# Reordering the gate entry, moving weight sums from GpSimd to VectorE, and another order for the output rows in a Winograd-multiplied transformer block

## The chip, the core and the metric

The kernel runs on one core of one Trainium2 chip. The core has five instruction streams that the profile names PE (TensorE, matrix products), DVE (VectorE, elementwise work), ACT (ScalarE, elementwise functions and casts), POOL (GpSimd, elementwise work) and SP (SyncE, which here issues the DMAs). Each works through its own list in order; they wait for each other through semaphores. The metric is the device time of one execution in microseconds (us), the median of several. The time before is 942.32 us (three runs, 941.96 to 943.43).

## The reference

One layer of a diffusion backbone over 1024 tokens with 1024 channels (cut):

```python
h = rms_norm(x, g_pre) * (1 + scale) + shift
q, k, v, g_a, u_f, g_f, c_a, c_b, g_c, s_a, s_f, s_c = split_in(h @ w_in)
attn = neighbourhood_attention(q, k, v, kc, vc, rpb)
y_a = (attn * silu(g_a)) @ p_attn
y_f = ((fourier_mix(u_f) @ w_four) * silu(g_f)) @ p_four
y_c = (conv_module(c_a, c_b, ...) * silu(g_c)) @ p_conv
merged = sigmoid(s_a) * y_a + sigmoid(s_f) * y_f + sigmoid(s_c) * y_c
x = x + gate * rms_norm(merged @ w_out, g_post)
```

All of it is float32. The change touches the last three stages: the gate products (`h @ w_in` for g_a, g_f, g_c and most of s_a, s_f, s_c), the projections by p_attn, p_four and p_conv with the merge, and the output product by w_out with its normalised rows.

## The kernel before, in words

A float32 product is made of three: each operand is split into a high and a low part in the type fp32r (`split`, L92: ACT casts the high part, DVE or POOL subtracts for the low one), and high x high, high x low and low x high are added up in PSUM (`mm3`). The channels lie on the 128 partitions in 8 tiles, the tokens in two halves of 512 columns.

**Gate stage** (from about 513 us). The weight columns of w_in come in pairs of 2 x 128 columns, `NP` = 12 pairs numbered 0 to 11. Of each pair the weights are a 2 x 2 block matrix a11, a12, a21, a22, and the activations are a 2 x 2 block matrix too, so that Winograd's form of Strassen's method makes the four output blocks from seven products, not eight. A product is 4 k-tiles x 3 = 12 matmuls of 128x512. It takes sums of weight blocks (`wsum`, L1260, tiles named w: w0 = a21+a22, w1 = w0-a11, w2 = a11-a21, w3 = a12-w1) and sums of activations (tiles t, made and split once by `h_sums`, `h_last` and `h_split`). `prep_a` to `prep_d` split a11 and a12, w0 and w1, w2 and w3, and a22, into tiles named c. `step` (L1335) holds the products p1 to p7 and the merges g2, g3, g4, g7:

- p1 fills the PSUM bank x; ACT copies it (s1). p2 fills y; g2 adds s1 and y on DVE.
- p6 adds into x; DVE copies it (u2, L1303). p7 adds into x again, so p7 cannot start before that copy, nor p6 before s1.
- p5 fills z; ACT copies it (s5). p3 adds into z, p4 fills a bank of its own. g7, g3 and g4 add copies and banks on DVE (L1329).

A merged gate goes through a tanh on ACT. The kind of a pair says what follows: for the first five pairs (kind "s") the tanh is stored to memory (`thd`, L1309); for pairs 5 to 7 (kind "g") DVE and POOL (L1325) multiply it into the branch results `mg`; for the last four (kind "a") it is kept in `mg`.

All five engines' orders are written by hand in this part: the order of the calls is the order on each engine. A call such as go(1, "p3", "g3") puts matmuls on PE, a copy on ACT and an addition on DVE at that place of each list. Pairs 0 to 2 are interleaved, as the activation sums become ready; pairs 3 to 11 go through a loop (L1482 and on). The raw weight tiles come through two buffers ("raw"), one for each half of a pair; `raws` issues the loads of the next pair as soon as the buffers' readers are placed. Up to pair 2 `wsum` runs on DVE, from pair 3 to 11 on POOL, after that on DVE.

**Projection** (from about 753 us). For each of 8 output tiles d and both halves h, three products are made; DVE multiplies each by its gate (L1633) and POOL adds the second and third into `mg[d]` (L1636), but for d = 7, h = 1, where DVE adds. Beside it `side` loads, combines and splits the weights w_out (tiles wo) for the last stage and loads the rows of the output gate.

**Output** (from about 843 us). The same seven-product form, with roles swapped: `mg` gives the blocks that are split into c tiles, w_out the sums. Four quarters n = NP to NP+3 of 2 x 128 tokens each. Here the merges are put on a list (`pend`) and `flush` hands them to `emit_out`: ACT squares and sums a row's half, POOL multiplies it by the output gate (L1724) and takes the power -0.5 (L1731), and DVE adds the scaled result to the rows of x (L1738), which SP stores. `x_load` loads those rows.

The end of the projection is written so that a11 of the first quarter is split in the projection's last step and a12 after it, in two pieces, since it needs the last tile of `mg`:

```python
a12 = mgt[1][:, :, 0:P]
dst = [v[:, 4:8] for v in ops["c0"]]
for ks in (slice(0, 3), slice(3, 4)):
    split(a12[:, ks], *(v[:, ks] for v in dst), dve)
```

Of the kernel before, what the change touches and what calls it, by code (L numbers as in the profile page):

```python
# [19 lines left out]
P = 128  # L20
# [32 lines left out]
def block_kernel(ctx: ExitStack, tc: tile.TileContext, x, ctxt, wmodp, wgate,  # L53
# [1206 lines left out]
    def wsum(n, i):  # L1260
        a11, a12, a21, a22 = blocks(n)
        i0, i1, op = ((a21, a22, ALU.add), (ops.get((n, 0)), a11, ALU.subtract), (a11, a21, ALU.subtract),
                      (a12, ops.get((n, 1)), ALU.subtract))[i]
        t = swp.tile([P, 512], F32, tag="sw", name=f"w{i}")
        t = t.rearrange("p (k c) -> p k c", k=4)
        (pool if 2 < n < NP else dve).tensor_tensor(out=t, in0=i0, in1=i1, op=op)  # L1266
        ops[n, i] = t

    def prep_b(n, which=(0, 1)):
# [188 lines left out]
    go(0, "g3")  # L1458
    go(1, "p7")
    prep_b(2, (1, 0))  # L1460
    h_split(4, 0, 1)
    go(0, "g7")
    go(1, "p3", "g3")
    h_last(2)
    h_last(3)
    go(2, "p1", "p2")
    h_split(4, 2, 3)
    go(1, "g7")
    for r in (6, 7, 4, 5, 0, 1):
        sp.dma_start(mg[r], fcd[r])  # L1470
    go(2, "p6", "g2")
# [151 lines left out]
    def project(d):  # L1623
        wh, wl = wget(i_p[d])
        for h in range(2):
            s = H[h]
            thq[d, 0, h] = mg[d][:, s]
            for b, (k0, k1) in enumerate(((0, 4), (4, 6), (6, 8))):
                ps = bank("ps")
                for k in range(k0, k1):  # L1630
                    mm3(ps, wh[:, k], wl[:, k], gh[k][:, s], gl[k][:, s], k == k0, k == k1 - 1)
                t = thq[d, b, h]
                dve.scalar_tensor_tensor(out=t, in0=t, scalar=1.0, in1=ps, op0=ALU.add, op1=ALU.mult)  # L1633
                if b > 0:
                    eng = dve if d == 7 and h == 1 else pool
                    eng.tensor_tensor(out=mg[d][:, s], in0=mg[d][:, s], in1=t, op=ALU.add)  # L1636
            side(d, h)

    def side(d, h):
# [29 lines left out]
        if (d, h) == (7, 0):  # L1669
            wload(7)  # L1670
            c0 = wtile("c0o")
            put(NP, "a11", mgt[0][:, :, 0:P], c0, 0)
            ops["c0"] = c0
            wsum(NP, 2)
        for i in WS.get((d, h), ()):
            wsplit(i)
# [26 lines left out]
    def emit_out(n, i, h, src):  # L1703
# [27 lines left out]
        pool.tensor_tensor(out=rs, in0=v, in1=mhalf, op=ALU.pow)  # L1731
        xt = xts[n, i]

        def end(h, eng=dve):
            s = H[h]
            y = yrow[t, h]
            if eng is dve:
                dve.scalar_tensor_tensor(out=xt[:, s], in0=y, scalar=rs, in1=xt[:, s], op0=ALU.mult, op1=ALU.add)  # L1738
            else:
                act.activation(y, y, AF.Identity, scale=rs)  # L1740
                pool.tensor_tensor(out=xt[:, s], in0=xt[:, s], in1=y, op=ALU.add)
            sp.dma_start(out[t * P:(t + 1) * P, s], xt[:, s])

        end(1 - h)
        if (n, i) == (NP + 3, 0):
            ends.append(lambda: end(h, pool))
            return
        while ends:
            ends.pop()()
        end(h)  # L1750

    ends = []
    n = NP
    a12 = mgt[1][:, :, 0:P]
    dst = [v[:, 4:8] for v in ops["c0"]]
    for ks in (slice(0, 3), slice(3, 4)):
        split(a12[:, ks], *(v[:, ks] for v in dst), dve)
    ops[n, "a12"] = dst
    wsum(n, 0)
    go(n, "p1")  # L1760
    prep_b(n, (0,))
# [27 lines left out]
    go(n, "p4")  # L1789
    prep_c(n + 1)  # L1790
    go(n + 1, "p1")
    flush()
    prep_d(n + 1)
    for n in range(NP + 1, NP + 4):
        more = n + 1 < NP + 4
        x_load(n)
        go(n, "p2", "g2")
        go(n, "p6")
        if more:
            prep_a(n + 1)  # L1800
            wsum(n + 1, 0)
            wsum(n + 1, 1)
        flush()
        go(n, "p5")
        go(n, "p7")
        if more:
            prep_b(n + 1)
            wsum(n + 1, 2)
# [10 lines left out]
        if more:  # L1819
            prep_d(n + 1)  # L1820
            go(n + 1, "p1")
        flush()
    allman.close()
    ds.close()
    ms_.close()
# [65 lines left out]
```

## Time and profile before

| what | value |
|---|---|
| median of 3 runs | 942.32 us |
| profiled execution, its own time | 943.67 us |
| its span, first to last instruction | 941.9 us |
| PE busy | 890.4 us, 95% |
| weight loads (PEld) busy | 746.4 us, 79% |
| DVE busy | 725.9 us, 77% |
| ACT busy | 413.8 us, 44% |
| POOL busy | 341.9 us, 36% |
| mean granted TensorE clock | 0.985 |

A row of the timeline gives the start, the duration, the engine, the source line, the operation and the tiles (written <- read), and in brackets how long the engine was idle before it and what ended that. Two operations of one kind that follow each other are merged (x2). A row of a table of stretches gives the stretch, its length, the busy time of the engines asked for with their counts, the granted clock of TensorE, the share of the DMA engines that were busy and GB/s. PE's busy time is modelled: matmuls follow each other closer than their durations say.

### The profile page before, as it was taken

What the parts mean: (1) busy time and instruction counts of PE and PEld (TensorE: products, weight loads), DVE (VectorE), ACT (ScalarE), POOL (GpSimd) and SP (SyncE); (2) the same over time, 40 slices, a digit from 0 to 9 for tenths busy, and PEclk for the clock granted to TensorE, in tenths of its full rate; (3) what the DMA queues carried; (4) which work ended last, traced back from release to release, by engine and by line L of the source; (5) the groups of instructions that cost most, each with busy time, mean ns of one, the idle gap of its engine ahead of it and who ended that gap; (6) DMA issues with size and microseconds to landing.
All of it is one profiled execution on the core that took longest, in us unless ns stands there. A gap on an engine that the chain in (4) does not pass through costs nothing. (4 is left out here: it accounts for less than half of the span.)

```text
span 941.9 us, 13235 instructions
## 1 busy us (share of the span) xinstructions
PE 890.4 (95%) x4652; PEld 746.4 (79%) x4652; DVE 725.9 (77%) x1183; ACT 413.8 (44%) x830; POOL 341.9 (36%) x310
## 2 busy tenths in 40 slices
PE   4899989999899999999999989999999999998896
PEld 2578889988678888888888877788878888775685
DVE  4656897596768999999959786557864679997985
ACT  4344523233456766776643444333343521225441
POOL 2123822164234434444420003335652048570232
PEclk9999989999999999999999999999999999999999
DMA  9703024345434444544323236423313799851323
GB/s 366 277 13 122 23 78 147 112 140 181 119 104 146 135 145 128 162 128 134 124 79 114 72 130 230 126 80 109 112 58 88 245 349 328 288 204 40 109 90 134
DMA packets 114162, 135.85 MB, mean 144 GB/s; under 512 B 5680, under 2 KB 83760, under 8 KB 114096
## 3 DMA queue, kind: packets, MB, share of 16 engines
q1 hardware_dynamic: 113952, 134.43, 43.5%
q0 software_dynamic: 144, 0.59, 0.3%
q8 instruction: 36, 0.59, 0.3%
q14 instruction: 30, 0.25, 0.1%
HBM read 102.03 MB, written 29.36 MB: 139 GB/s over the span
## 5 line engine op out<-in xcount | busy, mean ns | idle before, releaser
L141 PE MATMUL ps<-hh,whi 128*128 128x512 f32 x304 | 126.7, 417 | 0.9 <-DVE qd L851 0.9
L93 POOL TENSOR_TENSOR wlo<-raw,whi 128x512 fp32r<-128x512 f32 (+2 forms) x52 | 79.1, 1539 | 119.5 <-ACT whi L93 107.3
L143 PE MATMUL ps<-hh,wlo 128*128 128x512 f32 x304 | 119.6, 394 | 0.0
L142 PE MATMUL ps<-hl,whi 128*128 128x512 f32 x304 | 119.6, 393 | 0.0
L93 DVE TENSOR_TENSOR c<-w,c 128x512 fp32r<-128x512 f32 x64 | 53.0, 865 | 30.0 <-ACT c L93 29.9
L93 ACT CAST whi<-raw 128x512 fp32r<-128x512 f32 (+2 forms) x65 | 43.8, 705 | 69.7 <-PE ps L142 27.9
L1636 POOL TENSOR_TENSOR mg<-mg,th 128x512 f32<-128x512 f32 x30 | 50.6, 1687 | 62.3 <-DVE th L1633 60.7
L1013 POOL TENSOR_TENSOR bias<-mk,braw 128x288 f32<-128x288 bf16 (+1 forms) x64 | 54.2, 848 | 38.8 <-DVE mn L1045 37.6
L143 PEld LDWEIGHTS ps<-hh,wlo 128*128 128x128 f32 x304 | 57.5, 189 | 12.7
L141 PEld LDWEIGHTS ps<-hh,whi 128*128 128x128 f32 x304 | 57.7, 190 | 11.1 <-PE ps L143 1.3
L142 PEld LDWEIGHTS ps<-hl,whi 128*128 128x128 f32 x304 | 57.8, 190 | 9.7 <-issue 0.5
L1078 ACT CAST pt<-tp 96x384 fp32r<-96x384 f32 (+1 forms) x96 | 46.1, 514 | 43.0 <-PE tp L1071 42.3
L1084 DVE TENSOR_TENSOR pt<-tp,pt 96x384 fp32r<-96x384 f32 (+1 forms) x96 | 54.4, 593 | 2.9 <-ACT pt L1078 1.4
L1045 DVE CUSTOM_DVE_ANT_0 pr<-scb,bias 128x544 f32<-128x544 f32 (+1 forms) x64 | 49.4, 772 | 8.5 <-PE scb L1038 7.7
L1266 POOL TENSOR_TENSOR w<-raw 128x512 f32<-128x512 f32 x9 | 13.8, 1538 | 109.6 <-DMA raw<-in_w_in_dram 99.6
L1052 ACT ACTIVATE pr<-pr,mn 128x544 f32<-128x544 f32 (+1 forms) x64 | 50.8, 794 | 3.7 <-DVE mn L1045 3.6
L143 PE MATMUL ps<-gh,wlo 128*128 128x512 f32 x128 | 50.0, 390 | 0.7 <-DVE wlo L93 0.7
L141 PE MATMUL ps<-gh,whi 128*128 128x512 f32 x128 | 50.3, 393 | 0.0
L142 PE MATMUL ps<-gl,whi 128*128 128x512 f32 x128 | 50.0, 390 | 0.2 <-DVE gl L93 0.2
L1071 PE MATMUL tp<-ident,pr 128*128 128x128 f32 (+1 forms) x320 | 45.8, 274 | 1.4 <-DVE rc L1058 1.0
L93 ACT CAST c<-w 128x512 fp32r<-128x512 f32 x64 | 37.1, 617 | 22.7 <-DVE w L1266 19.5
L141 PE MATMUL x<-t,c 128*128 128x512 f32 x96 | 39.1, 407 | 6.5 <-ACT s L1301 3.3
(498 smaller groups left out, 2639.3 us busy)
## 6 DMA issues: line engine op xcount, KB each, us to landing
raw<-in_w_in_dram SPq DMA_DIRECT2D x51, 512.0 KB
wt<-in_wmodp_dram SPq DMA_DIRECT2D x16, 512.0 KB
thd<-th SPq DMA_DIRECT2D x32, 256.0 KB
th<-thd SPq DMA_DIRECT2D x32, 256.0 KB
braw<-in_rpbp_dram SPq DMA_DIRECT2D x32, 192.0 KB
vt<-vd SPq DMA_DIRECT2D x48, 128.0 KB
vd<-vs SPq DMA_DIRECT2D x20, 256.0 KB
vt<-vd SPq DMA_DIRECT2D x48, 96.0 KB
```

Source lines behind the costliest of these rows:

```text
L93: return act.copy(hi, src), (lo_eng or pool).tensor_tensor(out=lo, in0=src, in1=f32(hi), op=ALU.subtract)
L141: pe.matmul(ps, wh, mh, start=start, stop=False, **kw)
L142: pe.matmul(ps, wh, ml, start=False, stop=False, **kw)
L143: pe.matmul(ps, wl, mh, start=False, stop=stop, **kw)
L1013: pool.tensor_tensor(out=dst, in0=mk[:, a * 3 + MJ[j], 0:n].rearrange("p (r w) -> p r w", w=W), in1=raws[h_, min(j, 1)][:, :, 0:W], op=ALU ...
L1045: dve.tensor_tensor_reduce(out=pr, in0=sc, in1=biases[h_][:, FULL[h_](n)], scale=1.0, scalar=BIG, op0=ALU.add, op1=ALU.min, accum_out=mn)
L1052: act.activation(pr, pr, AF.Exp, scale=-1.0, bias=mn, accum_out=sums)
L1071: pe.transpose(tp[0:(kw if b < 3 else P), b], src, ident)
L1078: act.copy(pt[0:q, b0:b1, 0], tp[0:q, b0:b1])
L1084: dve.tensor_tensor(out=pt[0:q, b0:b1, 1], in0=tp[0:q, b0:b1], in1=f32(pt[0:q, b0:b1, 0]), op=ALU.subtract)
L1266: (pool if 2 < n < NP else dve).tensor_tensor(out=t, in0=i0, in1=i1, op=op)
L1636: eng.tensor_tensor(out=mg[d][:, s], in0=mg[d][:, s], in1=t, op=ALU.add)
```

## The change

Five edits:

1. Gate entry: the call for g7 of pair 0 and p3 of pair 1 goes ahead of the first half of the last activation split; p1 and p2 of pair 2 go ahead of g3 and g7 of pair 1; the second half of that split goes behind g7 of pair 1.
2. `wsum` runs on DVE for every pair.
3. In the projection DVE adds the parts for both halves of d = 7.
4. a12 of the first output quarter is split whole, inside the projection's last step.
5. Output rows: both halves of a row are finished by DVE one after the other; the special path through ACT and POOL for one row of the last quarter is gone; p6 with its copy is called ahead of the merge g2, and `flush` is called behind p6 and p7 and no more behind the next quarter's p1.

```diff
-        (pool if 2 < n < NP else dve).tensor_tensor(out=t, in0=i0, in1=i1, op=op)
+        dve.tensor_tensor(out=t, in0=i0, in1=i1, op=op)
...
     prep_b(2, (1, 0))
+    go(0, "g7")
+    go(1, "p3")
     h_split(4, 0, 1)
-    go(0, "g7")
-    go(1, "p3", "g3")
+    go(2, "p1", "p2")
+    go(1, "g3")
     h_last(2)
     h_last(3)
-    go(2, "p1", "p2")
+    go(1, "g7")
     h_split(4, 2, 3)
-    go(1, "g7")
...
-                    eng = dve if d == 7 and h == 1 else pool
+                    eng = dve if d == 7 else pool
...
             put(NP, "a11", mgt[0][:, :, 0:P], c0, 0)
-            ops["c0"] = c0
+            put(NP, "a12", mgt[1][:, :, 0:P], c0, 1)
             wsum(NP, 2)
...
-        end(1 - h)
-        if (n, i) == (NP + 3, 0):
-            ends.append(lambda: end(h, pool))
-            return
-        while ends:
-            ends.pop()()
-        end(h)
+        for s, y in ((H[v], yrow[t, v]) for v in (1 - h, h)):
+            dve.scalar_tensor_tensor(out=xt[:, s], in0=y, scalar=rs, in1=xt[:, s], op0=ALU.mult, op1=ALU.add)
             sp.dma_start(out[t * P:(t + 1) * P, s], xt[:, s])
...
     go(n + 1, "p1")
-    flush()
     prep_d(n + 1)
     for n in range(NP + 1, NP + 4):
         more = n + 1 < NP + 4
+        go(n, "p2", "p6", "g2")
+        flush()
         x_load(n)
-        go(n, "p2", "g2")
-        go(n, "p6")
         if more:
             prep_a(n + 1)
             wsum(n + 1, 0)
             wsum(n + 1, 1)
-        flush()
         go(n, "p5")
         go(n, "p7")
+        flush()
...
             go(n + 1, "p1")
-        flush()
+        else:
+            flush()
```

The lists of PE and SP keep their order. Three places of the others follow, each a piece of the difference between the two lists (a plus marks a row of the changed kernel, a minus one of the kernel before).

ACT at the gate entry: c are pair 2's weight splits, t the activation split, s the copies of PSUM banks (from x the copy s1 of pair 2, from z the copy s5 of pair 0), th the tanh of a merged gate (of s for g7 of pair 0, of u for g3 of pair 1):

```order
 L93 CAST c_6095<-w_6070 128x512
+L1301 COPY s_6101<-z 128x512
+L1308 ACTIVATE th<-s_6101 128x512
 L93 CAST t_5675<-mg_5657 128x512 x2
-L1301 COPY s_6105<-z 128x512
-L1308 ACTIVATE th<-s_6105 128x512
+L1301 COPY s_6136<-x 128x512
 L1308 ACTIVATE th<-u_6035 128x512
-L1301 COPY s_6144<-x 128x512
```

The copy of x stood behind both tanhs and now stands ahead of the second one; the two casts of t are now behind the first tanh.

DVE in the loop, at pair 3 (the same in every later pair): the merge g2, the low parts of a11 and a12 of pair 4 (c from raw), the sums w, the low part of a22 of pair 4, the copy u after p6 of pair 3:

```order
 L93 TENSOR_TENSOR c_6374<-raw_6315,c_6373 128x512 x2
+L1266 TENSOR_TENSOR w_6379<-raw_6317 128x512
+L1266 TENSOR_TENSOR w_6381<-w_6379,raw_6315 128x512
 L93 TENSOR_TENSOR c_6396<-raw_6317,c_6396 128x512
 L1303 COPY u_6411<-x 128x512
+L1266 TENSOR_TENSOR w_6413<-raw_6315,raw_6317 128x512
+L1266 TENSOR_TENSOR w_6415<-raw_6315,w_6381 128x512
 L93 TENSOR_TENSOR c_6437<-w_6379,c_6436 128x512
```

Four rows come in, two of them ahead of the copy u.

DVE in the second output quarter. Before:

```order
L1715 SCALAR_TENSOR_TENSOR v<-ssum,v 128x1
L1719 TENSOR_TENSOR y<-x,ggb 128x512
L1738 SCALAR_TENSOR_TENSOR xt<-u_8548,rs,xt 128x512
L1738 SCALAR_TENSOR_TENSOR xt<-y,rs,xt 128x512
L93 TENSOR_TENSOR c_8651<-mg_5657,c_8651 128x512
L1329 TENSOR_TENSOR s_8633<-s_8633,y 128x512
L1303 COPY u_8684<-x 128x512
```

And now:

```order
L93 TENSOR_TENSOR c_8633<-mg_5657,c_8633 128x512
L1303 COPY u_8661<-x 128x512
L1329 TENSOR_TENSOR s_8631<-s_8631,y 128x512
L1713 TENSOR_SCALAR v<-ssum 128x1
L1716 SCALAR_TENSOR_TENSOR v<-ssum,v 128x1
L1720 TENSOR_TENSOR y<-x,ggb 128x512
L1736 SCALAR_TENSOR_TENSOR xt<-u_8546,rs,xt 128x512
L1736 SCALAR_TENSOR_TENSOR xt<-y,rs,xt 128x512
```

The copy u after the quarter's p6 stood behind the rows' ends (xt) and now stands ahead of them.

More of the change, by code (lines that the diff above doesn't have):

```diff
@@ L1732, in emit_out @@
         xt = xts[n, i]
[L1734 to L1741, printed above, removed]
-            sp.dma_start(out[t * P:(t + 1) * P, s], xt[:, s])
-        end(1 - h)
-        if (n, i) == (NP + 3, 0):
-            ends.append(lambda: end(h, pool))
-            return
-        while ends:
-            ends.pop()()
-        end(h)
-    ends = []
-    n = NP
[L1754 to L1758, printed above, removed]
+        for s, y in ((H[v], yrow[t, v]) for v in (1 - h, h)):
+            dve.scalar_tensor_tensor(out=xt[:, s], in0=y, scalar=rs, in1=xt[:, s], op0=ALU.mult, op1=ALU.add)
+            sp.dma_start(out[t * P:(t + 1) * P, s], xt[:, s])
+    n = NP
     wsum(n, 0)
```

## The prediction

> **What bounds the kernel now.** I read the page first, then what TensorE (PE) waited for from the gate stage on, then the two engines that release it.
>
> ```profile
> PE 890.4 (95%) x4652; PEld 746.4 (79%) x4652; DVE 725.9 (77%) x1183; ACT 413.8 (44%) x830; POOL 341.9 (36%) x310
> 601.76:620.80 19.04, 19.04 (x85) 15.78 (x84) 8.71 (x13) 7.70 (x15) 2.93 (x2) 1.00 0.35 110
> 658.88:677.92 19.04, 18.72 (x83) 15.15 (x82) 15.48 (x17) 6.91 (x13) 11.78 (x8) 1.00 0.34 110
> ```
>
> PE is the bound. The lower two rows are stretches of one pair (after the length: busy PE, weight loads, DVE, ACT, POOL). Seven products fill 19.04 us, so a product lasts 2.72 us. The order of PE's products is the same before and after, so time can come only out of PE's stops. The timeline of PE has these (in brackets the idle time and what ended it):
>
> ```profile
> 554.36 0.50 PE L141 MATMUL x<-t,c 128*128 128x512 f32 x1 [2.67 <-ACT s L1301]
> 591.85 0.50 PE L141 MATMUL x<-t,c 128*128 128x512 f32 x1 [2.05 <-DVE u L1303]
> 670.27 0.50 PE L141 MATMUL x<-t,c 128*128 128x512 f32 x1 [0.32 <-DVE u L1303]
> 690.45 0.50 PE L141 MATMUL x<-t,c 128*128 128x512 f32 x1 [0.83 <-DVE u L1303]
> 849.25 0.80 PE L143 MATMUL y<-wo,c0o 128*128 128x512 f32 x1 [2.41 <-DVE c0o L93]
> 885.67 0.50 PE L141 MATMUL x<-wo,c 128*128 128x512 f32 x1 [2.15 <-DVE u L1303]
> ```
>
> A long stop costs twice, as stretches laid on the clock's own steps show (length, busy PE, granted clock):
>
> ```profile
> 583.25:586.66 3.41, 2.81 (x12) 1.00 0.86 254
> 589.82:593.24 3.42, 1.39 (x6) 1.00 0.00 0
> 593.24:596.65 3.41, 3.41 (x10) 0.50 0.95 265
> 845.82:849.23 3.41, 1.02 (x5) 1.00 0.84 319
> 849.23:852.65 3.42, 3.40 (x8) 0.50 0.01 4
> 886.78:890.19 3.41, 3.41 (x10) 0.50 0.59 192
> ```
>
> A stretch in which PE was busy for 1.39 or 1.02 us is followed by one of 3.41 us at half clock, which loses 3.41/2 = 1.7 us. A stretch with 2.81 us of work is not. The starts of the half-clock stretches (593.24, 849.23, 886.78) lie whole multiples of 3.41 apart, so where a stop falls on that grid matters too. The stops of 2.05 and 2.15 us are therefore worth about 3.75 and 3.85.
>
> The Trainium skill, "TensorE: Matmul & The Clock Gate", Part 1, says that the clock falls back after at least one idle window of about 3.4 us. By that rule no stop here would cost a half-clock stretch; the rows disagree, since 2.05 us was enough, and the measurement decides.
>
> **The weight sums, POOL to DVE.** Rows of pair 3, the first whose sums POOL makes:
>
> ```profile
> 572.25 1.14 ACT L93 CAST c<-raw 128x512 fp32r<-128x512 f32 x2 [1.04 <-DMA raw<-in_w_in_dram]
> 574.01 1.33 POOL L1266 TENSOR_TENSOR w<-raw 128x512 f32<-128x512 f32 x1 [81.42 <-DMA raw<-in_w_in_dram]
> 574.11 1.78 DVE L1329 TENSOR_TENSOR s<-s,u 128x512 f32<-128x512 f32 x1
> 576.00 0.69 DVE L1329 TENSOR_TENSOR u<-u,w 128x512 f32<-128x512 f32 x1
> 577.95 0.91 DVE L93 TENSOR_TENSOR c<-raw,c 128x512 fp32r<-128x512 f32 x1 [1.26 <-ACT c L93]
> 578.78 2.39 DVE L93 TENSOR_TENSOR c<-w,c 128x512 fp32r<-128x512 f32 x2
> 581.10 0.68 DVE L1329 TENSOR_TENSOR u<-u,z 128x512 f32<-128x512 f32 x1
> 583.42 0.58 ACT L1301 COPY s<-x 128x512 f32<-128x512 f32 x1
> 585.97 1.30 POOL L1266 TENSOR_TENSOR w<-raw 128x512 f32<-128x512 f32 x1 [5.95 <-DMA raw<-in_w_in_dram]
> 586.12 5.07 DVE L93 TENSOR_TENSOR c<-raw,c 128x512 fp32r<-128x512 f32 x3 [1.21 <-ACT c L93]
> 591.12 0.68 DVE L1303 COPY u<-x 128x512 f32<-128x512 f32 x1
> L1266 POOL TENSOR_TENSOR w<-raw,w x9: 1297/1716/1762, 578.3 to 719.6; 128x512 f32<-128x512 f32 x9
> L1266 DVE TENSOR_TENSOR w<-raw x3: 684/684/685, 510.4 to 544.2; 128x512 f32<-128x512 f32 x3
> ```
>
> A sum takes POOL up to 1.7 us and DVE 0.68. DVE's operation at 574.11 has the shape of the one at 576.00, starts while POOL runs, and takes 1.78 us instead of 0.69; the three splits at 586.12 take 5.07 us beside four POOL sums instead of three times 0.69. So a sum on POOL costs DVE about 1.1 us, more than the 0.69 of doing it itself.
>
> The Trainium skill, "SBUF — State Buffer", Who interferes with whom, has the cause: a DVE operation with two SBUF inputs and a GpSimd one that reads SBUF exclude each other for a whole instruction. The Trainium skill, "Perfetto Trace Analysis", Optimizing Scalar/DVE Operations, would offload a saturated DVE even to GpSimd, which speaks against this change, but doubts that it helps between these two; 5.07 us for three splits bears out the doubt.
>
> The walk for pair 3: DVE at 574.11, then 0.69 + 0.69 for the merges, 4 x 0.69 for the sums, 0.69 for a22's split, 1.29 for two splits and 0.68 for u<-u,z give 580.9, against 581.78 before. ACT follows with a tanh, two casts and the copy (583.42 before), so PE starts product 6 about 0.9 earlier, near 583.1. Products 6 and 5 end at 588.6. DVE meanwhile merges s<-s,y to 583.9; ACT's tanh (0.63) and first cast (0.6) end at 585.2; two splits end at 586.45, two sums at 587.8, a22's split at 588.5 and the copy at 589.2. Product 7 starts there and not at 591.85: **2.65 us**. The 0.6 us that is left of that stop asks for no half clock: **1.7 us** more. The tiles stay landed in time: the first two rows carry the DMA's time, and I keep 572.25 and 574.01.
>
> In the later pairs DVE gains 4 x 0.69 = 2.75 us of work, and has 19.04 - 15.48 = 3.56 us free even in the fuller row, with POOL's sums still in its way. The stops of 0.32 and 0.83 go: **1.15 us**. If POOL's gate multiplications (four in a pair of that kind) delay DVE as much as the sums did, this term is zero, not negative, by that 3.56.
>
> **The gate entry.**
>
> ```profile
> 549.87 1.14 ACT L93 CAST t<-mg 128x512 fp32r<-128x512 f32 x2
> 553.20 0.63 ACT L1308 ACTIVATE th<-u 128x512 f32<-128x512 f32 x1
> 553.74 0.57 ACT L1301 COPY s<-x 128x512 f32<-128x512 f32 x1
> ```
>
> One tanh of 0.63 us leaves the queue ahead of the copy that ends the stop at 554.36; the two casts stay ahead of it, after the first tanh instead of before. The copy ends near 553.55, so the stop shrinks by 0.7 us, and by 1.7 more if the grid spares it. I count **0**: PE then reaches pair 3 early, where DVE's walk hangs on tiles that land at 572.25 and 574.01, and waits for the same 583.1. The moved splits of quarters 2 and 3 now stand behind the last tanh and end near 560.2 (an estimate: nine DVE rows of 0.69 from 551.4 on and three waits for ACT); product 4 of pair 0 reaches the third quarter at 553.6 + 5.44 + 1.36 = 560.4. Bounds: -0.5 (that product waits) and +0.9 (the tiles land that much earlier).
>
> **The end of the projection.**
>
> ```profile
> 841.26 1.40 DVE L93 TENSOR_TENSOR c0o<-mg,c0o 128x512 fp32r<-128x512 f32 x1
> 848.64 0.75 DVE L93 TENSOR_TENSOR c0o<-mg,c0o 128x384 fp32r<-128x384 f32 x2
> 849.32 0.68 DVE L1266 TENSOR_TENSOR w<-mg,mg 128x512 f32<-128x512 f32 x1
> 850.68 0.69 DVE L93 TENSOR_TENSOR c<-w,c 128x512 fp32r<-128x512 f32 x1 [0.69 <-ACT c L93]
> 857.74 1.23 DVE L93 TENSOR_TENSOR wo<-wl,wo 128x1024 fp32r<-128x1024 f32 x1 [2.29 <-ACT wo L93]
> 858.89 0.69 DVE L1303 COPY u<-x 128x512 f32<-128x512 f32 x1
> ```
>
> Two POOL merges become two DVE ones of 0.69. The split of a11 at 841.26 moves behind them, to 843.3, just ahead of product 1; a12's follows, to 844.1 rather than 849.39 (848.64 + 0.75). So product 2, which stopped at 846.84 and went on at 849.25, runs through to 848.95. The stop moves to product 5, whose operand's low half still ends at 851.37 (850.68 + 0.69; DVE has the same work up to there). Ten of its twelve matmuls of 2.72/12 us follow, and it ends near 853.7. ACT's copy of it and the cast behind that (0.6 + 1.0) end near 855.4, and DVE, with its earlier work done at 855.45, no longer waits its 2.29 us: the split ends at 856.8 and the copy that releases product 7 at 857.5, instead of 859.58: **2.1 us**. After it the weight splits on DVE pace PE as before.
>
> **Half clock at the new stops.** PE now stops about 1.7 us ahead of pair 3's product 6 and some 2 us around product 5 here. Inside one stretch they leave 1.4 to 1.7 us busy, nearest to the 1.39 that was punished; split over two stretches they leave over 2.4, nearer to the 2.81 that was not. Bounds 0 and 1.7 + 1.1 us (at pair 3 the 0.6 left ahead of product 7 takes up the rest). I charge **-0.85**, half of one.
>
> **Output rows.** In the second quarter, the copy that releases product 7 stood behind two merges of output rows; it now stands right after product 6. It needs product 6 alone, which ends a whole product 5 (2.72 us) before the stop begins, so the stop at 885.67 goes: 2.15 + 1.7 = **3.85 us**. The output work now stands between this copy and the next one: a merge 0.69, scalars, a product 0.68, two rows of 0.75 with a wait for POOL's multiplication of about 1.0, two splits 1.29, two sums 1.38 and the copy 0.69, some 7.4 us, where PE allows three products, 8.16. A little more contention eats that in three quarters: I charge **-0.6**, bounds 0 and -2. The tail:
>
> ```profile
> 935.55 1.74 DVE L1738 SCALAR_TENSOR_TENSOR xt<-u,rs,xt 128x512 f32<-128x512 f32 x1
> 937.21 0.74 DVE L1738 SCALAR_TENSOR_TENSOR xt<-y,rs,xt 128x512 f32<-128x512 f32 x1
> ```
>
> The row at 935.55 loses the POOL addition that it shares time with (1.74 becomes 0.75), and waits a little longer for the row put ahead of it: the last ends near 937.15 instead of 937.95, **0.8 us**.
>
> **The sum.** 2.65 + 1.7 + 1.15 + 0 + 2.1 - 0.85 + 3.85 - 0.6 + 0.8 = 10.8 us. The profiled execution took 943.67 us (span 941.9 and 1.8 around it), which gives 932.9; it stood 1.35 above the median of 942.32, so the forecast is **931.5 us**.
>
> **Rivals.**
> *The projection swallows the gate's gain.* It runs close to two other bounds:
>
> ```profile
> 760.00:800.00 40.00, 40.00 (x178) 33.15 (x177) 35.67 (x36) 4.32 (x5) 29.49 (x16) 1.00 0.97 350
> ```
>
> DVE is 35.67 of 40 us busy and the DMA engines 0.97. Against it: its loads are issued behind PE's and DVE's progress, so they move up too. It would take back 2.65 + 1.7 + 1.15 = 5.5 us: 937.0. Chance 0.1.
> *The half clock does not come from the stops* and comes at as many places as before: the 1.7 at pair 3, at the projection and at 885.67 is not won. 931.5 + 5.1 - 0.85 = 935.8. Against it stand the busy times of 1.39 and 1.02 ahead of the half clock. 0.07. The rule of the Trainium skill's "TensorE: Matmul & The Clock Gate", Part 1, under which stops of 2 us cost no clock, would be this case.
> *DVE gains nothing from POOL's absence*, because POOL's other operations still hold it: two sums of 0.69 stand ahead of each copy for product 7, so 1.38 is added at four pairs, with one more half clock, 7.2 us, and the gate's 5.5 is not won: 944.2, no change to slightly slower. The 2.05 us of idle under 5.07 us of splits speaks against it. 0.03.
> *Slower, by a tile.* DVE runs in order, so the sum that reads a pair's second weight tile now stops the split and the copy behind it until that tile has landed. A tile is released some 14 us before DVE asks for it (19.04 less the some 5 us from a pair's first sum to its last); the one that POOL awaited at 585.97 landed 7 us after its buffer's last reader (the split at 577.95) was done. Beyond 14 us each microsecond costs up to one in nine pairs: at 17 us, 27 us, so 959. 0.02.
>
> **How the numbers follow.** The forecast, with anything from none to both of the new half clocks (930.7 to 933.5), has 0.75; its own range is 929 to 934. The rivals have 0.22 and 0.03 is left. From 928 (bounds of the entry and of the charges in its favour) to 936.5 the range leaves out most of the first rival and the last two. A measurement of this kernel tells 0.2%, some 1.9 us, from none: faster 0.94, same 0.03, slower 0.03.
>
> **What would show it.** No POOL sum between 570 and 720 and no DVE split of three over 2.2 us there; product 7 of pair 3 starting within 0.7 us of product 5's end; product 2 of the first output quarter without a stop, and a stop of 1.5 to 2 us ahead of product 5; no stop ahead of the second quarter's product 7. Wrong would be a copy waiting behind a sum whose tile has not landed, a stop at product 4 of the later quarters over 0.7 us, or PE waiting in the projection where it did not.

## The result, and the profile after

The changed kernel takes 935.08 us (median of 4 runs, 932.58 to 936.78) beside 942.88 us (941.96 to 944.37) of the kernel before: ratio 0.9896, interval 0.9868 to 0.9923, by which some 9.8 us are won. The two medians, of four runs each, differ by 7.8 us; three of the four runs of the kernel before are those of the 942.32. Measured again beside the experiments, with 6 runs against 17, it took 934.74 us against 944.32: ratio 0.9894 (0.9873 to 0.9916), and 9.6 us between the medians. The forecast was faster, 931.5 us, within 928.0 to 936.5. The profiled execution took 936.78 us (span 935.0).

The busy times on the page after:

```profile
PE 888.6 (95%) x4652; PEld 744.1 (80%) x4652; DVE 729.6 (78%) x1221; ACT 412.7 (44%) x828; POOL 283.3 (30%) x271
```

36 sums of 0.68 us, 24.6 us, moved onto VectorE (DVE), yet its busy time grew by 3.7 us only. The groups of DVE between 570 and 720 us show why. First the kernel before, then the changed one (busy us and mean ns stand behind the bar):

```profile
L93 DVE TENSOR_TENSOR c<-w,c 128x512 fp32r<-128x512 f32 x32 | 28.8, 940 | 20.2 <-ACT c L93 20.2
L93 DVE TENSOR_TENSOR c<-raw,c 128x512 fp32r<-128x512 f32 x24 | 28.2, 1217 | 8.7 <-ACT c L93 8.6
L1303 DVE COPY u<-x 128x512 f32<-128x512 f32 x15 | 10.3, 685 | 9.4 <-PE x L143 9.4
L1329 DVE TENSOR_TENSOR s<-s,u 128x512 f32<-128x512 f32 x8 | 6.7, 836 | 0.2
L1329 DVE TENSOR_TENSOR u<-u,w 128x512 f32<-128x512 f32 x8 | 5.5, 685 | 0.2
```

```profile
L93 DVE TENSOR_TENSOR c<-w,c 128x512 fp32r<-128x512 f32 x32 | 24.0, 790 | 15.4 <-ACT c L93 15.4
L93 DVE TENSOR_TENSOR c<-raw,c 128x512 fp32r<-128x512 f32 x24 | 19.1, 824 | 9.7 <-ACT c L93 9.7
L1303 DVE COPY u<-x 128x512 f32<-128x512 f32 x15 | 10.3, 689 | 4.5 <-PE x L143 4.5
...
L1329 DVE TENSOR_TENSOR s<-s,u 128x512 f32<-128x512 f32 x8 | 5.5, 691 | 0.2
L1266 DVE TENSOR_TENSOR w<-raw,w 128x512 f32<-128x512 f32 x8 | 5.5, 684 | 0.0
```

The same splits take 13.9 us less once the sums have left GpSimd (POOL). The copy out of PSUM, a DVE operation with one input, takes 685 and 689 ns: it never was slowed. Nor was the addition u<-u,w, where w is the PSUM bank of product 4: 685 ns in the kernel before, though 6 of the 8 ran beside a POOL operation. The addition s<-s,u, with both inputs in SBUF, goes from 836 to 691. So in these groups only operations with two inputs in SBUF were held up.

How they are held up is seen in the single splits of the trace. Of these splits, 22 took over 0.9 us in the kernel before, and each of the 22 ended 0.55 us after the end of a POOL operation, as if the split ran only when that operation was done. In the changed kernel 6 are left, up to 1.79 us long, all beside the gate multiplications that stay on POOL, and they too end 0.54 to 0.55 us after one. They bring no stop.

The places of TensorE (PE) that the prediction spoke of, in the timeline after (in brackets the stop ahead and what ended it; no bracket, no stop):

```profile
558.28 0.50 PE L141 MATMUL x<-t,c 128*128 128x512 f32 x1 [1.96 <-ACT s L1301]
...
587.64 0.50 PE L141 MATMUL x<-t,c 128*128 128x512 f32 x1 [1.11 <-ACT s L1301]
...
593.60 0.50 PE L141 MATMUL x<-t,c 128*128 128x512 f32 x1 [0.22 <-DVE u L1303]
...
670.20 0.50 PE L141 MATMUL x<-t,c 128*128 128x512 f32 x1
...
849.48 0.50 PE L141 MATMUL z<-wo,c 128*128 128x512 f32 x1 [1.57 <-ACT c L93]
...
881.57 0.39 PE L141 MATMUL x<-wo,c 128*128 128x512 f32 x1
```

Product 7 of pair 3 stops for 0.22 us instead of 2.05, the row at 670 not at all, product 7 of the second output quarter not at all. The 2.41 us ahead of the first quarter's product 2 have become 1.57 us ahead of its product 5. In front of pair 3's product 7, DVE's work is what the walk had said:

```profile
589.72 1.29 DVE L93 TENSOR_TENSOR c<-raw,c 128x512 fp32r<-128x512 f32 x2 [1.21 <-ACT c L93]
590.93 0.68 DVE L1266 TENSOR_TENSOR w<-raw 128x512 f32<-128x512 f32 x1
591.64 0.69 DVE L1266 TENSOR_TENSOR w<-w,raw 128x512 f32<-128x512 f32 x1
592.25 0.68 DVE L93 TENSOR_TENSOR c<-raw,c 128x512 fp32r<-128x512 f32 x1
592.86 0.68 DVE L1303 COPY u<-x 128x512 f32<-128x512 f32 x1
```

PE's list of matmuls is the same in both kernels, so the start of each can be compared. The table has how far each stretch of the program was shortened, from the same matmuls of the profile before; the second column of measured values is the changed kernel's second profile. The boundaries are given in the time of the kernel before.

| stretch (us, before) | forecast | after | second profile |
|---|---|---|---|
| start to 540, not touched by the change | 0 | +4.6 | +1.9 |
| gate entry to pair 3's product 7 (540 to 598.5) | -4.35 | -4.5 | -4.8 |
| later pairs (to 700) | -1.15 | -1.3 | -1.35 |
| projection (to 846) | 0 | 0.0 | 0.0 |
| first output quarter (to 859.6) | -1.25 | -0.6 | -0.6 |
| second quarter (to 890.5) | -3.85 | -4.1 | -4.0 |
| third and fourth (to 930) | +0.6 | +0.5 | +0.5 |
| tail | -0.8 | -1.5 | -1.3 |
| sum from 540 on | -10.8 | -11.5 | -11.6 |

In the ten profiles of other kernels that leave the first 540 us alone, this part ends 0.7 to 5.5 us later than in the profile before. Where that comes from is told under "When a stop costs half clock".

### The profile page after: what moved, and what is told of

Same layout as the page of the kernel before. It is cut to its first block, busy times and chain, and to the rows that moved or that the text cites. A ratio compares the mean times of both kernels' runs of the same rounds, so it can differ in the third digit from the quotient of the medians.

```text
span 935.0 us, 13198 instructions
## 1 busy us (share of the span) xinstructions
PE 888.6 (95%) x4652; PEld 744.1 (80%) x4652; DVE 729.6 (78%) x1221; ACT 412.7 (44%) x828; POOL 283.3 (30%) x271
## 5 line engine op out<-in xcount | busy, mean ns | idle before, releaser
L1637 POOL TENSOR_TENSOR mg<-mg,th 128x512 f32<-128x512 f32 x28 | 47.6, 1701 | 99.8 <-DVE th L1634 98.4
L1325 POOL TENSOR_TENSOR mg<-mg,th 128x512 f32<-128x512 f32 x12 | 17.7, 1471 | 167.1 <-DVE th L1324 167.1
L93 DVE TENSOR_TENSOR c<-w,c 128x512 fp32r<-128x512 f32 x64 | 46.0, 756 | 22.5 <-ACT c L93 22.4
L1059 DVE TENSOR_SCALAR pr<-pr,rc 128x544 f32<-128x544 f32 (+1 forms) x64 | 41.7, 652 | 2.3
```

Source lines behind the costliest of these rows:

```text
L93: return act.copy(hi, src), (lo_eng or pool).tensor_tensor(out=lo, in0=src, in1=f32(hi), op=ALU.subtract)
L1059: dve.tensor_scalar(out=pr, in0=pr, scalar1=rc, scalar2=None, op0=ALU.mult)
```

## The experiments

Theory: a GpSimd operation on SBUF holds up a VectorE operation with two inputs there for more than the sum's own 0.69 us, so the sums' place decides the gate; the order of the output rows removes a stop of its own; a stop of some 2 us can bring a half-clock stretch behind it. Rivals: the sums are only relocated; the parts need or take each other's gain; half clock comes whatever PE does.

### The weight sums alone

```diff
-        (pool if 2 < n < NP else dve).tensor_tensor(out=t, in0=i0, in1=i1, op=op)
+        dve.tensor_tensor(out=t, in0=i0, in1=i1, op=op)
```

> The weight sums of all gate pairs on VectorE, nothing else changed. Theory (a sum on GpSimd costs VectorE more than doing it itself): about 5.5 us faster than the kernel before, 4.35 of it at pair 3 (the stop of 2.05 us ahead of its product 7 shrinks below 1.3 us and the half-clock stretch behind it goes) and 1.15 at the stops near 670 and 690; each VectorE sum 0.69 us, each pair of splits 1.29 us, none beside a GpSimd sum. Rival one (VectorE gains nothing from GpSimd's absence, the work is only moved): no faster, to 7 us slower, with splits still at 1.7 us. Rival two (the gain at the gate needs the new order of the gate entry as well): 1 to 2 us faster, with the stop ahead of pair 3's product 7 still at about 2 us. The half-clock stretch of the first output quarter near 849 stays under all of them.

Measured: 938.75 us against 945.05, ratio 0.9935 (0.9923 to 0.9947), some 6.1 us. The PE timeline of this run, at the gate entry and at pair 3's product 7:

```profile
557.48 0.50 PE L141 MATMUL x<-t,c 128*128 128x512 f32 x1 [2.68 <-ACT s L1301]
...
592.14 0.50 PE L141 MATMUL x<-t,c 128*128 128x512 f32 x1
```

The entry's stop of 2.7 us is still there, and product 7 does not stop at all. By the starts of its matmuls, pair 3 was won with 4.45 us and the later pairs with 1.35, as forecast, without the new entry. The theory holds; both rivals fall.

### GpSimd's sums back as ghosts

```diff
+        dve.tensor_tensor(out=t, in0=i0, in1=i1, op=op)
+        if 2 < n < NP:
+            g = swp.tile([P, 512], F32, tag="sw", name="ghost")
+            pool.tensor_tensor(out=g.rearrange("p (k c) -> p k c", k=4), in0=i0, in1=i1, op=op)
```

> The weight sums of the gate pairs on VectorE as in the run with the sums alone, and GpSimd makes each sum a second time into a buffer that nobody reads. Theory (VectorE and GpSimd hold each other up whenever both work on SBUF): VectorE's sums and splits there go back to 1.3 to 1.8 us each where a ghost runs beside them, the stop ahead of pair 3's product 7 is 2 us or more again and stops come at product 7 of later pairs; the gain of the sums is gone, and with four sums more on VectorE it is 0 to 4 us slower than the kernel before. Rival (the gain came from the place of the sums in VectorE's order, not from GpSimd's absence): within 1 us of the run with the sums alone, 5 to 7 us faster than the kernel before.

Measured: 951.81 us against 944.32, ratio 1.0075 (1.0056 to 1.0095): 7 us slower than the kernel before and 13 slower than the sums alone. Nobody reads a ghost. DVE's groups between 570 and 720 us and PE's stops in this run:

```profile
L93 DVE TENSOR_TENSOR c<-raw,c 128x512 fp32r<-128x512 f32 x24 | 26.7, 1141 | 8.8 <-ACT c L93 8.8
...
L1266 DVE TENSOR_TENSOR w<-raw,raw 128x512 f32<-128x512 f32 x8 | 9.9, 1243 | 0.0
...
L1306 DVE COPY u<-x 128x512 f32<-128x512 f32 x14 | 9.6, 685 | 3.4 <-PE x L143 3.4
...
L1266 DVE TENSOR_TENSOR w<-raw,w 128x512 f32<-128x512 f32 x8 | 5.4, 681 | 1.2 <-POOL ghost L1269 1.2
```

```profile
586.15 0.50 PE L143 MATMUL w<-t,c 128*128 128x512 f32 x1 [2.68 <-DVE c L93]
...
598.30 0.50 PE L141 MATMUL x<-t,c 128*128 128x512 f32 x1 [2.21 <-DVE u L1306]
...
659.28 0.50 PE L141 MATMUL x<-t,c 128*128 128x512 f32 x1 [2.14 <-DVE u L1306]
...
680.78 0.50 PE L141 MATMUL x<-t,c 128*128 128x512 f32 x1 [2.17 <-DVE u L1306]
```

The splits are back at 1.14 us, two of the sums take 1.23 and 1.24 instead of 0.68 us, and stops of 2.1 to 2.2 us stand at product 7 of three pairs. The edit also has a cost of its own: the ghosts need buffers, and DVE waited 1.2 us for one of them (last row of the groups). That wait stands ahead of the split that ends the first stop shown, of 2.68 us, which has a half-clock stretch behind it. So up to some 2.9 us (1.2 and 1.7) of the 13 may come from the buffers and not from the contention. At the later pairs no such wait stands. The theory's sign and mechanism hold; its size (0 to 4 us slower) was too small, by the stops of 2 us at later pairs, where the kernel before had 0.3 and 0.8, and by this wait. "Whenever both work on SBUF" was too wide: the copy takes 685 ns here as well. This is the case that the Trainium skill, "SBUF — State Buffer", Who interferes with whom, describes for VectorE operations with two SBUF inputs beside GpSimd ones that read SBUF, and the runs agree: 0.68 us alone, 1.24 on average for a sum that ghosts run beside.

### Half of the sums on GpSimd

```diff
-        dve.tensor_tensor(out=t, in0=i0, in1=i1, op=op)
+        (pool if 2 < n < NP and i > 1 else dve).tensor_tensor(out=t, in0=i0, in1=i1, op=op)
```

> The changed kernel with two of a pair's four weight sums (the third and fourth, which are made beside the splits ahead of product 7's copy) back on GpSimd. Theory (what counts is what shares time with VectorE ahead of the copies that release products; of the 2.65 us at pair 3 about 0.9 were won ahead of product 6 and 1.75 after it): the splits beside the two sums go back to 1.3 to 1.8 us each, the stop ahead of pair 3's product 7 to 1 to 1.8 us, and the stops near 670 and 690 come back in part: 2 to 4 us slower than the changed kernel, 6 to 8 faster than the kernel before. Rival (only the first two sums, which share time with the merges, matter): within 1 us of the changed kernel.

Measured: 939.69 us against 945.24, ratio 0.9943 (0.9918 to 0.9968); about half of the change's gain is gone. PE's stops in this run:

```profile
594.04 0.50 PE L141 MATMUL x<-t,c 128*128 128x512 f32 x1 [1.22 <-DVE u L1303]
...
652.79 0.50 PE L141 MATMUL x<-t,c 128*128 128x512 f32 x1 [1.01 <-DVE u L1303]
...
673.16 0.50 PE L141 MATMUL x<-t,c 128*128 128x512 f32 x1 [1.02 <-DVE u L1303]
```

The two sums that stand beside the splits ahead of product 7 cost 1.22 us at pair 3, and 1 us at two later pairs, where they were expected. The size was too small again: by the ratios this is 5.4 us faster than the kernel before, where 6 to 8 were expected, and some 4.5 slower than the changed kernel, where 2 to 4 were. The other half of the sums was not tried alone.

### The gate entry alone, and everything but the entry

```diff
+    go(0, "g7")
+    go(1, "p3")
     h_split(4, 0, 1)
-    go(0, "g7")
-    go(1, "p3", "g3")
+    go(2, "p1", "p2")
+    go(1, "g3")
...
```

> The new order of the gate entry alone. Theory (pair 3 waits for the same tiles and the same VectorE walk, so what the entry wins is given back there): within 0.5 us of the kernel before, the stop of 2.67 us ahead of pair 2's product 6 down by about 0.7 us, and the stops ahead of pair 3's product 1, 6 or 7 longer by what it won (2.4 if the half-clock stretch near 555 goes with it). Rival (the entry's gain is carried through): 0.7 to 2.4 us faster.

> The changed kernel with the old order of the gate entry: the weight sums, the end of the projection and the output rows are changed, the entry is not. Theory (pair 3 waits for its tiles and for VectorE's walk either way, so the entry's gain is given back there, half clock included): within 1.3 us of the changed kernel, 8.5 to 10.5 us faster than the kernel before, with a longer stop (2.7 us) ahead of pair 2's product 6 and shorter ones ahead of pair 3's product 6. Rival (the 0.3% that the entry gave alone is carried through): 2 to 3 us slower than the changed kernel.

The entry alone: 944.02 us against 945.05, ratio 0.9970 (0.9952 to 0.9988). Everything but the entry: 935.31 us against 945.24, ratio 0.9901 (0.9864 to 0.9938), no different from the full change's 0.9894. PE's stops of the entry alone:

```profile
554.32 0.50 PE L141 MATMUL x<-t,c 128*128 128x512 f32 x1 [1.88 <-ACT s L1301]
...
585.07 0.50 PE L141 MATMUL x<-t,c 128*128 128x512 f32 x1 [2.37 <-ACT s L1301]
...
592.70 0.50 PE L141 MATMUL x<-t,c 128*128 128x512 f32 x1 [1.89 <-DVE u L1303]
```

The first stop is 0.8 us shorter and has no half clock behind it, and the stop ahead of pair 3's product 6, which had been 0.60 us, is 2.37. By the starts, the execution was 2.4 us ahead at 561 us and where it had been before the entry (+0.8) at 598 us. With the changed sums and the old entry, the stops are 2.75 and 1.13 us: there too the gate is won with 4.3 us. So this profile shows the gain swallowed at pair 3, as forecast; the 0.3% that the timed runs of the entry alone show, with single times from 937.5 to 945.7 us, is not explained by it and does not come back in the whole. What it is stays open.

### The output rows alone

```diff
-        if (n, i) == (NP + 3, 0):
-            ends.append(lambda: end(h, pool))
...
+        go(n, "p2", "p6", "g2")
+        flush()
         x_load(n)
-        go(n, "p2", "g2")
-        go(n, "p6")
...
         go(n, "p7")
+        flush()
```

> The new order of the output quarters and of the rows' ends alone. Theory: 3.85 at the second quarter (the stop of 2.15 us ahead of its product 7 and the half-clock stretch behind it go), some 0.3 to 0.6 given back at later stops, 0.8 to 1.4 at the tail: 4.3 to 5.0 us faster than the kernel before. Rival (the half-clock stretches are not caused by the stops and come as often): 1.7 less, 2.6 to 3.3 us faster, with a half-clock stretch in the second quarter that no stop stands ahead of. The first output quarter is as before, its stop of 2.4 us and its half-clock stretch with it.

Measured: 939.82 us against 945.05, ratio 0.9949 (0.9937 to 0.9961), some 4.8 us. Product 7 of the second quarter:

```profile
885.05 0.39 PE L141 MATMUL x<-wo,c 128*128 128x512 f32 x1
```

No stop stands ahead of it. By the starts, 2.3 us of stop and 1.7 of half clock went there, 0.3 came back by 895 us, and the tail gave 1.5. As expected.

In this run the first quarter kept its stop, and yet had no half clock. The row, then its grid stretch and the next (length, busy PE, weight loads, DVE, ACT, POOL, granted clock):

```profile
852.55 0.50 PE L143 MATMUL y<-wo,c0o 128*128 128x512 f32 x1 [2.40 <-DVE c0o L93]
```

```profile
850.71:854.12 3.41, 1.57 (x7) 1.31 (x8) 2.69 (x6) 0.79 (x2) 0.00 (x0) 1.00 0.37 144
854.12:857.53 3.41, 3.41 (x17) 2.82 (x16) 3.41 (x5) 2.36 (x3) 0.00 (x0) 1.00 0.04 11
```

1.57 us of work in the stretch, and the next ran at full clock; the kernel before had 1.02 us there with a stop of 2.41, and paid. What differs is where the stop fell on the grid.

### The end of the projection alone

```diff
-                    eng = dve if d == 7 and h == 1 else pool
+                    eng = dve if d == 7 else pool
...
-            ops["c0"] = c0
+            put(NP, "a12", mgt[1][:, :, 0:P], c0, 1)
...
```

> The last merges of the projection on VectorE and the split of a12 put ahead of the output quarters, nothing else. Theory: product 2 of the first output quarter loses its stop of 2.4 us, product 5 gets one of 1.5 to 2 us, and the half-clock stretch comes or stays away with the busy time of the grid stretch in which the new stop falls: 0.4 us faster than the kernel before with a half-clock stretch at about 850, 2.1 without. Rival (stop and half clock only move, and the weight splits on VectorE that follow give the rest back): within 0.3 us of the kernel before.

Measured: 944.03 us against 945.05, ratio 0.9997 (0.9981 to 1.0014): no difference. Product 5 of the first output quarter:

```profile
854.10 0.50 PE L141 MATMUL z<-wo,c 128*128 128x512 f32 x1 [1.58 <-ACT c L93]
```

The stop of 2.4 us is gone from product 2, and 1.58 us stand ahead of product 5, whose first matmuls follow each other more slowly: by the starts 2.6 us are won and 2.1 given back. The profile has no half clock here, where the profile before had 1.7 us of it, so this quarter is 2.2 us shorter in it. The expected 0.4 and the rival's 0.3 both lie inside the interval of the timed runs, which cannot tell them apart; 2.1 lies outside.

### Matmuls of no use in the stops

```diff
+    FILL = {(2, "s2"): 6, (3, "s3"): 6, (NP, "a12"): 6, (NP + 1, "s3"): 6}
...
+        if (n, a) in FILL:
+            if not start:
+                spare.append(bank("f"))
+            for _ in range(FILL[n, a]):
+                pe.matmul(ps if start else spare[0], f[:, 0:P], f, start=True, stop=True, skip_group_check=True)
...
```

> The kernel before with six matmuls of 128x512 (6 x 0.23 = 1.4 us) of no use put on TensorE ahead of the products that stop at 554, 592, 849 and 886 us; they run while it would stand. Their results are overwritten or dropped. Theory (half clock follows from too little work in one stretch of the 3.41 us grid): the waits end when they did, but no half-clock stretch comes at any of the four places; where the profiles so far had one in about half of the cases at 1.7 us each, this is 2 to 4 us faster than the kernel before, with less spread. Rival (half clock comes whatever TensorE does there): the same time as the kernel before, with half-clock stretches at some of these places.

Measured: 942.33 us against 944.32, ratio 0.9980 (0.9965 to 0.9996). PE around pair 3:

```profile
588.43 0.50 PE L141 MATMUL x<-t,c 128*128 128x512 f32 x1 [2.10 <-ACT s L1310]
...
594.02 1.52 PE L1299 MATMUL f<-hh 128*128 128x512 f32 x6
...
596.32 0.50 PE L141 MATMUL x<-t,c 128*128 128x512 f32 x1 [0.77 <-DVE u L1312]
```

No half-clock stretch lies between 540 and 900 us in this profile. The half clock that was saved at the entry came back as a longer wait at pair 3's product 6 (2.10 us), the same swallowing as above. Nothing waits any less than before, and PE does useless work in addition, yet the kernel is 2 us faster. That speaks for the theory, though one profile without half clock at the four places could also be luck, and 2 us is the low end of what was expected.

### When a stop costs half clock

All half-clock stretches of one profile start on one grid of 3.413 us, to 0.03 us, and the grid lies elsewhere in each execution. Over all 14 profiles, between 36 and 920 us, I sorted the full-clock stretches of this grid by PE's busy time in them:

| busy PE in the stretch of 3.41 us | stretches | followed by half clock |
|---|---|---|
| up to 1.54 us | 39 | 39 |
| 1.55 to 1.90 us | 23 | 8 |
| over 1.90 us | 3473 | 1 |

The one in the last row holds matmuls of 128x2, which may take PE's time and little of its work; that was not tried. In the band between, busy time alone does not decide, and what does was not found. An example is the first output quarter in the changed kernel's profile:

```profile
847.46:850.87 3.41, 1.84 (x7) 0.90 (x7) 2.62 (x5) 1.65 (x3) 0.00 (x0) 1.00 0.10 40
850.87:854.29 3.42, 3.42 (x10) 2.65 (x9) 3.35 (x4) 1.49 (x2) 0.00 (x0) 0.50 0.40 115
```

1.84 us busy, and the next stretch is at half clock. So a stop of 1.9 to 2.75 us pays only when most of it falls into one stretch: in the profiles that have such a stop at one of the four places unchanged or nearly so, 9 of 21 did. The profile before paid at all four. The new stop of 1.54 to 1.59 us ahead of product 5 paid in 4 of 6 profiles.

The Trainium skill, "TensorE: Matmul & The Clock Gate", Part 1, says that the window is about 3.4 us long and free-running. The grid of 3.413 us and its changing phase agree. It also speaks of an idle window as the condition; 1.54 us of work in it, 45%, did not protect.

The same chance moves the first 540 us, which the change leaves alone. Against the profile before, the ten other profiles that have this part unchanged are shifted at four places: ahead of 18 us (by 0.1 to 1.6 us; the granted clock first reaches 1.00 at 16.4 us in the profile before and at 16.8 to 19.5 in the others), at 25 to 36 (0 or 1.6), at 118 to 142 (0 to 3.1) and at 240 to 252 (0 to 2.0). Between these places a shift is 0.6 us at most. At the last three the profiles differ in their half-clock stretches. The profile after, at the third:

```profile
123.64 0.44 PE L141 MATMUL ps<-h_wf,h_bs 128*128 128x256 f32 x1 [3.67 <-DVE wcl L93]
...
135.92 0.38 PE L142 MATMUL ps<-wlo,hh 128*128 128x256 f32 x1 [2.49 <-DVE wlo L93]
```

The first stop is as long in the profile before. There 6.83 us at half clock follow it, and no second stop. Here 3.41 us follow, PE comes sooner to the next thing that it awaits from DVE, stops for 2.49 us, and has another 3.41 us at half clock behind that. No run moves the grid by itself, so that its place is the cause is argued from these places and not tested.

### Further along the same way

Since the untouched first part has stops of 3.7 us at 123 and of 2.5 us at 245 with half clock behind them in every profile, three kernels put ready work or useless matmuls there, on top of the change.

```diff
-            adv(2)
+            adv(4 if (si, k) == (0, 1) else 2)
...
-        adv((2, 2)[h])
+        adv((4, 2)[h])
```

> The changed kernel with work that is ready put ahead of two products that wait at about 120 us (stop of 3.67 us) and 244 us (2.4 to 2.7 us), in a part of the program that the change leaves alone. Theory (each of these stops has a half-clock stretch of 3.4 to 6.8 us behind it in every profile so far, worth 1.7 to 3.4 us): the stops shrink below 1 us and the half-clock stretches there go: 5 to 9 us faster than the changed kernel in the same runs. Rival (VectorE, which the waits are for, is the bound there, and the stop only comes later): no faster than 2 us.

Measured: 930.11 us (928.73 to 931.91) against 944.32, ratio 0.9851 (0.9831 to 0.9871), 4.6 us under the changed kernel's 934.74 in the same runs, and the best of all. Its stops in the first part:

```profile
133.73 0.58 PE L142 MATMUL ps<-wlo,hh 128*128 128x256 f32 x1 [4.58 <-DVE wlo L93]
...
277.07 0.39 PE L1035 MATMUL scb<-kctx,qd 128*128 128x256 f32 x1 [1.98 <-DVE mn L1045]
```

The stop at 123 only moved to 133 and grew to 4.58 us, with 6.8 us of half clock: the rival is right there. The one at 245 went, and 1.98 us came at 277 with half clock. So neither stop shrank as the theory says, and yet more than the rival's 2 us was won. By the starts, this profile is 1.7 us ahead of the changed kernel's second one at 540 us, and another 1.6 of the 3.6 us between the two is the half-clock stretch of the first output quarter, which did not come; the edit does not act there.

The next left the first place alone, took less at the second (`(3, 2)`), and put useless matmuls ahead of pair 2's product 6 and the first quarter's product 5:

```diff
-        adv((2, 2)[h])
+        adv((3, 2)[h])
...
+    FILL = {(2, "s2"): 6, (NP, "s1"): 5}
...
```

> The changed kernel with one piece of ready work put ahead of the product that waits at about 244 us, and with matmuls of no use (six and five of 128x512, 1.4 and 1.1 us, results dropped) ahead of pair 2's product 6 and product 5 of the first output quarter. Theory: the stop at 244 falls to about 1.2 us and its half-clock stretch of 3.4 to 6.8 us goes (3 to 4.5 us), the half-clock stretch of the first output quarter goes (1.7 us where it came), the one at the entry goes but is given back at pair 3: 4 to 6 us faster than the changed kernel, 929 to 931 beside a kernel before of 944. Rival (the work that is put ahead leaves a wait of the same size uncovered behind it): 1 to 2 us faster than the changed kernel.

Measured: 934.35 us against 945.24, ratio 0.9902 (0.9869 to 0.9934): no gain over the change. From 540 us on it has no half clock outside the tail. But behind the stop at 245, which fell to 1.23 us, a half-clock stretch came nevertheless, and a wait of 1.63 us stands at 280 us:

```profile
245.88 0.27 PE L918 MATMUL pv__2542<-omat,hi 128*128 128x2 f32 x1 [1.23 <-ACT hi L93]
...
280.13 0.39 PE L1035 MATMUL scb<-kctx,qd 128*128 128x256 f32 x1 [1.63 <-DVE mn L1045]
```

The rival describes it better than the theory. The last run kept this and handed the convolution's steps out more slowly:

```diff
+    tap["rate"] = 0.5
     fold(0)
...
         ae.append((fh, fl))
+        tap["rate"] = 1.0
```

> As the run before this one, and the convolution's steps are handed to VectorE at half the rate until the products that wait for it at 120 to 136 us are through (they are made up for later). Theory (VectorE's convolution steps stand ahead of the splits that these products wait for): the stop of 3.7 us at 123 shrinks below 1.9 us, its half-clock stretches of 3.4 to 6.8 us go, 3 to 6 us more. Rival (VectorE bounds this stage; the wait comes later, where the steps are made up for): within 2 us of the run before this one.

Measured: 930.81 us against 945.24, ratio 0.9863 (0.9831 to 0.9895). Two stops of this run:

```profile
121.08 0.39 PE L141 MATMUL ps<-h_wf,h_bs 128*128 128x256 f32 x1 [1.20 <-DVE wcl L93]
...
238.31 0.76 PE L141 MATMUL ps<-hh,whi 128*128 128x512 f32 x1 [4.85 <-DVE kst L548]
```

The stop at 121 is 1.2 us, without half clock, as expected; the convolution's steps that were put off cost 4.85 us at 238. Both readings have a share: some 3.5 us were won over the run before it.

## Why the prediction was right, point by point

**What bounds.** Right. PE's list did not change, and the gain came out of its stops, the half clock behind them, and the tail.

**The weight sums.** Right in mechanism and size: 2.65 + 1.7 forecast, 4.5 and 4.8 measured; the later stops 1.15 forecast, 1.3 measured. The ghosts show the mechanism, since they bring GpSimd's work back and leave DVE's as it is; of their 13 us, up to 2.9 may be their buffers'. One reading was off: the row at 576.00, taken as an operation that POOL does not hold up, ran beside a POOL sum too:

```profile
575.42 1.63 POOL L1266 TENSOR_TENSOR w<-w,raw 128x512 f32<-128x512 f32 x1
```

Its second input is a PSUM bank, and that is why it took 0.69 us; the 0.69 holds all the same, since s<-s,u takes 691 ns in the changed kernel. One step inside was off: the stop ahead of pair 3's product 6 is 1.11 us and not 1.7, because part of the entry's gain (0.7 us by the starts) was already given back at pair 3's product 1. The end was the same. And no split of three over 2.2 us was seen, but two splits in a row still take up to 2.39 us beside POOL's gate multiplications.

**The gate entry, counted at 0.** Right in the profiles: with the old entry the gate is won as well. The bound of +0.9 was not reached in the whole; the 0.3% of the entry alone is not understood.

**The end of the projection.** Here the forecast failed in size: 2.1 - 0.85 = 1.25 us, where the changed kernel's profiles show 0.6 and the part alone nothing measurable. The step is "instead of 859.58". The walk to the copy at 857.5 was made at full clock and is right: in the run of the part alone, whose profile has no half clock here, this copy ends 2.2 us earlier against the matmuls of the projection, at 857.4 in the time of the kernel before. But the 859.58 contained a half-clock stretch of that execution. So 1.7 of the 2.1 was this stretch, and a charge of half of one for the new stop could not balance it where the new stop pays too, as it did in 4 of 6. With half clock on both sides 0.6 us is left, without it on either side 0.5 (2.6 less 2.1).

**Output rows.** 3.85 forecast, 4.1 and 4.0 measured, 1.7 of it the half clock of the profile before; 0.6 charged for contention, 0.5 measured. **Tail:** 0.8 forecast, 1.3 to 1.5 measured: the last row on DVE ends 0.7 us earlier against the rows before it, and the end behind it is 0.8 us shorter.

**The sum** of 10.8 stands against 11.5 in the profile and some 9.8 to 10 by the timed ratios (7.8 and 9.6 by the medians). The difference between these is where I chose badly: the sum was made against an execution that paid half clock at all four stops, and three of these stretches (5.1 us) are in it in full, one of them unseen. A typical execution pays at fewer than half of the places, so the part of the gain that is half clock is smaller on average. The start of 942.32, a median of three, was low besides: the kernel before gave 942.9 to 945.2 beside the later runs. Both made the forecast too low. Its own range (929 to 934) missed the median by a microsecond for these two reasons; the wide one held it. That 10.8 and the profile's 11.5 are so near is in part luck: the end of the projection gave 0.65 less than forecast, and the tail 0.5 to 0.7 more.

**Rivals.** The projection swallowed nothing (0.0 us between 700 and 846). That half clock does not come from the stops is refuted by the table of stretches, and the matmuls of no use agree. That DVE gains nothing is refuted by the sums alone. No copy waited behind a sum's tile: the sums' groups show no idle time for a DMA.

**The parts together.** Alone they give 0.65 + 0.30 + 0.51 + 0.03 = 1.5%, together 1.05%. Without the entry's 0.30 it is 1.2%, inside the intervals. Before its second measurement, the changed kernel was expected 10 to 12 us faster if the parts add up, and 7 to 8 if they take each other's gain; 9.6 by the medians and 10.0 by the ratio is at the edge of the first.

## What to carry to other kernels

Work moved from GpSimd to a VectorE that is three quarters busy can cost VectorE almost nothing (24.6 us of sums, 3.7 more busy) and end its longest delays: look whether its operations with two inputs in SBUF take twice as long while GpSimd works, and whether a copy, or an operation with one input in PSUM, does not. Price a half-clock stretch as a chance and not as a fact of one profile: mark the grid, see how much work is left in the stretch, and walk before and after at the same clock. A gain ahead of a wait for landed tiles or for another engine's walk is counted at zero until that wait is moved too.

## What the runs showed of the hardware that was not expected

Full and half clock are divided by a narrow band, 1.55 to 1.9 us of work in 3.41; 39 of 39 stretches below it were followed by half clock. The start of the grid against the program differs from execution to execution, and an untouched part of 540 us ended up to 5.5 us later, nearly all of it at places where the half-clock stretches differ or the clock first rises. A VectorE split that is held up by GpSimd ends 0.55 us after the GpSimd operation, in all 22 cases of the kernel before, and an addition with one input in PSUM is not held up at all (0.69 us). And useless matmuls in a wait made a kernel faster: 0.9980 (0.9965 to 0.9996).
